# RWKV mixer's end on one core: batch-norm statistics, a two-part second output, a quarter of the output product in fp32, gate weights on strips

## The chip, the cores and the metric

The kernel runs on one core of a Trainium2 chip. The metric is the device time of one execution in microseconds (us); lower is better. The engines are named as in the profile: PE is TensorE (matrix products and transposes), DVE is VectorE, ACT is ScalarE, POOL is GpSimd, SP issues most DMAs. The program is fixed: every engine works through its own list of instructions in order and waits for semaphores of the others.

## The reference

Two layers over 256 positions of width 1024, all in float32: layer 0 mixes positions by sparse attention (NSA), layer 1 by RWKV-7, and each is followed by a squared-ReLU MLP of width 4096. The change lies at the end of the RWKV mixer and at its entrance. Cut to what matters there:

```python
def rwkv7_mixer(h, v_first, x_mix, w_rkv, ..., g1, g2, k_k, k_a, r_k, ln_w, ln_b, w_out, v_res):
    dx = jnp.pad(h, ((0, 0), (1, 0), (0, 0)))[:, :-1] - h
    xr, xw, xk, xv, xa, xg = (h + dx * x_mix[i] for i in range(6))
    ...
    g = jax.nn.sigmoid(xg @ g1) @ g2                      # 1024 -> 160 -> 1024
    def step(state, inp):                                 # one position after the other
        sa = jnp.einsum('bhij,bhj->bhi', state, -kk_t)
        state = state * w_t[...] + sa[..., None] * (kk_t * a_t)[...] + v_t[..., None] * k_t[...]
        return state, jnp.einsum('bhij,bhj->bhi', state, r_t)
    y = ...                                               # (1, 256, 16 heads, 64)
    mu = jnp.mean(y, axis=-1, keepdims=True)
    var = jnp.mean(jnp.square(y - mu), axis=-1, keepdims=True)
    yn = ((y - mu) * lax.rsqrt(var + GN_EPS)).reshape(B, S, D) * ln_w + ln_b
    y = yn + bonus.reshape(B, S, D)
    return (y * g) @ w_out, v_first
```

## The kernel before

The 256 positions lie as two token tiles, t = 0 and t = 1, of 128 rows each. Weights come from memory in 188 chunks of 512 KB (`wchunk`, L224): SP issues the load into a ring of four buffers `wst`, ACT copies it to `wh` in the shortened format fp32r (L231), and DVE subtracts to get the rest `wl` (L233). A product with weights is then three fp32r products (`mm3`, L265: high by high L267, high by low L268, low by high L269). Products that need no split are plain fp32 (`mm`).

A scheduler places the instructions of PE, ACT, DVE and POOL from the program as written, within their dependences; `tc.issue_after(x)` keeps what is built inside it behind x. SP's list stays as written. Large tiles live in numbered slots (`big`, `done`, L240) and PSUM accumulators in a pool of four (`pacc`).

**Entrance.** `mlp` (L376) ends with its second product for the last four of 32 f-steps (the tail), first for t = 0, then for t = 1 one column block `cb` after the other. After each block `x` is updated (L430) and `after(t, cb)` of `rwkv_input` (L816) runs: it normalises x, transposes it (tile `hnp`, L833), and DVE makes `hn` and the shifted difference `dx`. For t = 1 it also builds the small products of decay and a (`lora`, L804, tile `pl`) and of the gate (`lora_g`, L810, tile `pg`, 160 columns), the gate's for both token tiles as hn·g1 + dx·(mix·g1). Later the gate rows are transposed to `gT` (L907 to L916), 128 and 32 of the 160 in separate parts.

**Middle.** `rwkv` works in four chunks of 64 positions, C = 64. `products` (L1109) makes the masked products M of a chunk. `gate_gemm` (L1137) makes g by one 128-row and one 32-row fp32 product of 512 columns for each of four blocks. Then the recurrence, for each chunk c: right sides Z (`right_sides`, tile pZ, copied to `Zt` by ACT), solution Q (`solve`, tile pQ, to `VS` by ACT), next state S (`next_state`, tile pS; DVE adds `w` and scales to `W`), and after two chunks the output Y of a token tile (`output`, tile pY, to `y` by ACT). A string lists the order in which they are built (L1330).

**End.** `group_norm(t)` (L1283) works in two halves of 512 columns: DVE sums, scales and subtracts the mean; ACT squares; DVE sums again; POOL takes the power -1/2; DVE multiplies by it, by `lnw`, adds `vt` and multiplies by `g`. PE transposes the half (`yTp`, L1305); ACT makes `yTh` (L1307), DVE `yTl` (L1308). `out_proj` (L329, called at L1341) multiplies by w_out in eight chunks (kh, cb), quarter kh and column block cb, six products each for a token tile, into `roa`. The last three chunks go to slots as `rowh`, `rowl`. Then x is updated (L367) and the next MLP's input is transposed (`m1p`) and split (`m1h`, `m1l`); its first product is `mu`.

Of the kernel before, what the change touches and what calls it, by code (L numbers as in the profile page):

```python
# [9 lines left out]
F32 = mybir.dt.float32  # L10
# [11 lines left out]
H = 16  # L22
# [153 lines left out]
def trunk(ctx: ExitStack, tc: tile.TileContext, wb, x_in, wg, cw1k, cw1v, cw2, vecs_in, l1, w2, a2, g2, rows,  # L176
# [45 lines left out]
    wnext = [0]  # L222

    def wchunk(pattern=None, alloc=None, **dims):  # L224
# [8 lines left out]
        V.tensor_tensor(wl, st, wh.bitcast(F32), op=ALU.subtract)  # L233
# [95 lines left out]
    def out_proj(hT, lT, name, after, tail=TAIL, hold=(), own=2):  # L329
# [9 lines left out]
        def part(kh, cb, t):  # L339
            if (kh, cb) not in wch:  # L340
# [6 lines left out]
            wh, wl = wch[kh, cb]  # L347
            for k in range(2):
                kk = kh * 2 + k
                sl = slice(t * 128, (t + 1) * 128)  # L350
                mm3(acc[t, cb], hT(kk, sl), lT(kk, sl), wh[:, k], wl[:, k], kk == 0, kk == KT - 1)
# [8 lines left out]
        for t in range(NT):  # L360

            rest = sorted(od[-tail:], key=lambda o: (o[0] > 1 and o[1] + 1, o)) if t else od[-tail:]
            for i, (kh, cb) in enumerate(rest):
                part(kh, cb, t)
# [11 lines left out]
    def mlp(hl, name, after, early=lambda: None):  # L376
        h, l = hl
        with tc.tile_pool(name=f"mlp{name}", bufs=1) as mp:
# [44 lines left out]
            for t in range(NT):  # L423
                for cbs in ((0,), (1,)) if t else ((0, 1),):
                    with tc.issue_after(m_.ins) if t else ExitStack():
                        for f in range(NF - TAIL, NF):
                            m_ = second(f, t, cbs)
                    for cb in cbs:
                        xs = x[:, t, cb * 512:(cb + 1) * 512]
                        V.scalar_tensor_tensor(xs, acc[t][cb], r2[:, t:t + 1], xs, op0=ALU.mult, op1=ALU.add)  # L430
                        after(t, cb)
# [356 lines left out]
    def rwkv_input(wts):  # L788
# [27 lines left out]
        def after(t, cb_):  # L816
# [13 lines left out]
            for i in range(2):  # L830
                p = pmm([128, 4, 128], "hnp")
                for j in range(4):
                    nc.tensor.transpose(p[:, j], xs[t][:, (4 * i + j) * 128:(4 * i + j + 1) * 128], ident)  # L833
# [5 lines left out]
            if t == 1:  # L839
                lora_g(0)  # L840
                lora(1)
                lora_g(1)
                done(l1a, m1a, g1, m1g)
# [15 lines left out]
    def rwkv(inp):  # L859
        hn, dx, xrh, xrl, w2t, a2t, lo = inp  # L860
        with ExitStack() as es:
# [45 lines left out]
            gT = pool.tile([128, 2, S], F32, name="gT")  # L907
            gs = sm.tile([128, NT, 160], F32, tag="gs", bufs=1, name="gs")
            act(gs, lo["pg"], AF.Tanh, scale=0.5)
            V.tensor_scalar(gs, gs, 0.5, 0.5, op0=ALU.mult, op1=ALU.add)  # L910
            p = pacc("pgT", [128, 2, NT, 128])
            for t in range(NT):
                nc.tensor.transpose(p[:, 0, t], gs[:, t, :128], ident)
                nc.tensor.transpose(p[:32, 1, t], gs[:, t, 128:], ident)
            act(gT[:, 0].rearrange("p (t q) -> p t q", t=NT), p[:, 0], AF.Copy)
            act(gT[:32, 1].rearrange("p (t q) -> p t q", t=NT), p[:32, 1], AF.Copy)  # L916

            def feature_tile(hT, lT, dst):
# [5 lines left out]
                act(dst, p, AF.Copy)  # L924

# [9 lines left out]
            xvh, xvl = split(V_MV, "xv")  # L935
            done(hn, dx)
# [196 lines left out]
            nc.sync.dma_start(gw[1][:32], g2[128:])  # L1133
# [3 lines left out]
            def gate_gemm(t):  # L1137
                sl = slice(t * 128, (t + 1) * 128)
                for cb in range(2):
# [277 lines left out]
```

## Time and profile before

| what | value |
|---|---|
| three runs | 734.05, 734.08, 735.78 us; median 734.08 |
| profiled execution, its own time | 735.48 us |
| its span on the core | 733.70 us |
| mean granted clock of TensorE | 0.989 of full speed |
| PE busy | 711.5 us, 97% of the span |
| DVE, ACT, POOL busy | 468.8, 432.0, 18.2 us |
| chain that ended last | PE 91%, DVE 4%, ACT 2%, issue 1%, DMA 1% |

The span is the time from the core's first to its last instruction in the profiled execution; what lies around it makes up the rest of that execution's time. Times inside the trace count from the start of the span. A busy share is an average over stages with different limits, so what is idle in a stage is read from that stage. A row of a timeline gives the start, the length, engine, line, operation, tiles and shapes; in brackets stand the idle time of that engine just before and what ended it. Matrix products overlap, so the time that one costs is the step from its start to the next one's, which is shorter than its length.

### The profile page before, as it was taken

To read this page: it belongs to the slowest core of one execution; us is meant where nothing else is said; L and a number is where in the kernel's file an instruction comes from. 1 tells how busy PE (TensorE), PEld (TensorE's weight loads), DVE (VectorE), ACT (ScalarE), POOL (GpSimd) and SP (SyncE) were. 2 spreads that over 40 slices of the span, in tenths; PEclk is the share of its full clock that TensorE was granted. 3 is DMA by queue.
4 is the path that set the end of the run, shared out by engine and by line. 5 is a ranking of instruction groups with operands and counts; after the bars stand their busy time and mean duration, and the time that the engine had idled before them with its cause. 6 is when DMAs were issued, how large, how long until landed. Compare 5 with 4: busy or idle time off the path is not lost.

```text
span 733.7 us, 13437 instructions
## 1 busy us (share of the span) xinstructions
PE 711.5 (97%) x5308; PEld 609.1 (83%) x5308; DVE 468.8 (64%) x960; ACT 432.0 (59%) x863; POOL 18.2 (2%) x34
## 2 busy tenths in 40 slices
PE   9999999999999999999999999996899999999996
PEld 7877776779898999898999987685689998899894
DVE  5765899548545454566875889987657454545454
ACT  6735688328555555565366896765157556555652
POOL 1000000000000000000000010001200000000000
PEclk9999999999999999999999999999799999999999
DMA  7947120126755555575025423052318555555531
GB/s 288 336 153 272 37 79 2 59 87 232 235 176 195 179 193 177 192 240 200 1 87 173 145 65 87 3 191 84 132 58 255 192 185 184 191 185 187 185 103 58
DMA packets 32012, 111.52 MB, mean 152 GB/s; under 512 B 3629, under 2 KB 4141, under 8 KB 31950
## 3 DMA queue, kind: packets, MB, share of 16 engines
q1 hardware_dynamic: 30878, 108.95, 44.0%
q10 hardware_dynamic: 928, 1.19, 0.7%
q8 instruction: 42, 0.69, 0.4%
q0 software_dynamic: 144, 0.52, 0.2%
q14 instruction: 20, 0.16, 0.1%
HBM read 108.55 MB, written 1.05 MB: 149 GB/s over the span
## 4 chain that ended last, share of the span: by engine, by line
PE 91%; DVE 4%; ACT 2%; issue 1%; DMA 1%; POOL 0%; SPq 0%; POOLq 0%; DVEq 0%
PE mu L267 8%; PE mu L268 8%; PE mu L269 8%; PE mo L267 8%; PE mo L269 8%; PE mo L268 8%; PE acc L268 4%; PE acc L269 4%; PE acc L267 4%; PE pa L269 2%; PE pa L268 2%; PE pa L267 2%; PE S L639 2%; PE po L683 1%; PE pM L1116 1%
## 5 line engine op out<-in xcount | busy, mean ns | idle before, releaser
L233 DVE TENSOR_TENSOR wl<-wst,wh 128x1024 fp32r<-128x1024 f32 x175 | 213.6, 1224 | 181.3 <-ACT wh L231 181.0
L231 ACT ACTIVATE wh<-wst 128x1024 fp32r<-128x1024 f32 x175 | 184.6, 1060 | 161.2 <-PE mu L268 77.5
L267 PE MATMUL mo<-wh,mqh 128*128 128x512 f32 x224 | 88.5, 397 | 0.0
L268 PE MATMUL mo<-wl,mqh 128*128 128x512 f32 x224 | 88.4, 395 | 0.0
L269 PE MATMUL mo<-wh,mql 128*128 128x512 f32 x224 | 87.4, 396 | 0.0
L267 PE MATMUL mu<-m0h,wh 128*128 128x256 f32 x256 | 72.5, 285 | 0.4 <-DVE m0l L305 0.4
L269 PE MATMUL mu<-m0h,wl 128*128 128x256 f32 x256 | 72.3, 283 | 0.0
L268 PE MATMUL mu<-m1l,wh 128*128 128x256 f32 x256 | 72.0, 282 | 0.0
L268 PE MATMUL mu<-m0l,wh 128*128 128x256 f32 x256 | 71.8, 282 | 0.0
L269 PE MATMUL mu<-m1h,wl 128*128 128x256 f32 x256 | 71.7, 281 | 0.0
L267 PE MATMUL mu<-m1h,wh 128*128 128x256 f32 x256 | 71.3, 282 | 0.0
L269 PEld LDWEIGHTS mo<-wh,mql 128*128 128x128 f32 x224 | 42.1, 188 | 10.3
L267 PEld LDWEIGHTS mu<-m0h,wh 128*128 128x128 f32 x256 | 48.2, 189 | 1.8 <-DVE m0l L305 0.6
L268 PEld LDWEIGHTS mu<-m0l,wh 128*128 128x128 f32 x256 | 48.4, 189 | 1.3 <-DVE m0l L305 0.2
L268 PEld LDWEIGHTS mu<-m1l,wh 128*128 128x128 f32 x256 | 48.2, 188 | 1.2
L267 PEld LDWEIGHTS mu<-m1h,wh 128*128 128x128 f32 x256 | 47.8, 188 | 1.2
L268 PEld LDWEIGHTS mo<-wl,mqh 128*128 128x128 f32 x224 | 42.2, 188 | 8.0
L267 PEld LDWEIGHTS mo<-wh,mqh 128*128 128x128 f32 x224 | 42.1, 188 | 7.7
L269 PEld LDWEIGHTS mu<-m1h,wl 128*128 128x128 f32 x256 | 48.2, 188 | 0.0
L269 PEld LDWEIGHTS mu<-m0h,wl 128*128 128x128 f32 x256 | 48.1, 188 | 0.0
L267 PE MATMUL acc<-wh,n0h 128*128 128x512 f32 x80 | 31.9, 405 | 0.1
L268 PE MATMUL acc<-wl,n0h 128*128 128x512 f32 x80 | 31.3, 397 | 0.2 <-DVE wl L233 0.2
(369 smaller groups left out, 1444.9 us busy)
## 6 DMA issues: line engine op xcount, KB each, us to landing
wst<-in_wb_dram SPq DMA_DIRECT2D x188, 512.0 KB, 3.7
w1t<-in_cw1k_dram SPq DMA_DIRECT2D x4, 512.0 KB, 6.1
w1t<-in_cw1v_dram SPq DMA_DIRECT2D x4, 512.0 KB, 7.1
x<-in_x_dram SPq DMA_DIRECT2D x4, 256.0 KB, 4.9
VS<-vt ACTq DMA_DIRECT2D x8, 128.0 KB, 4.7
out_dram<-xg SPq DMA_DIRECT2D x4, 256.0 KB, 2.2
g<-in_l_dram SPq DMA_DIRECT2D x2, 320.0 KB, 5.9
l1a<-in_l_dram SPq DMA_DIRECT2D x1, 512.0 KB
```

The costliest lines, as they stand in the source:

```text
L231: act(wh, st, AF.Copy)
L233: V.tensor_tensor(wl, st, wh.bitcast(F32), op=ALU.subtract)
L267: mm(o, lh, rh, start=first, stop=False)
L268: mm(o, lh, rl, start=False, stop=False)
L269: return mm(o, ll, rh, start=False, stop=last)
L639: mm(S1, qT[gp][:, hg, 128:256], kT[gp][:, s], start=True, stop=True)
L683: mm(po[s * 64:(s + 1) * 64, :S], vv[:, 0, vs], pt0[s][:, b], start=False, stop=False)
L1116: mm(p[s][:, j], head(BK, k0 + j, s, c).rearrange("p a s -> p (a s)"), head(AR, k0 + j, s, c).rearrange("p a s -> p (a s)"), start=True, s ...
```

## The change

Seven parts. (1) In the MLP's tail the hnp transposes of t = 0 are placed ahead of the last two f-steps of (t = 1, cb = 1). (2) The gate's small product of t = 1 is made from `xg` = hn + mix·dx, eight DVE operations and eight products instead of sixteen; the gate rows are transposed later, the 32 narrow ones onto four strips of 32 rows. (3) `gate_gemm` lists the four full products and then the four 32-row ones, each in rows of its own. (4) The order string and the holds change, and Y of the second token tile is built in two parts with the first tile's group norm between. (5) Group norm takes its statistics by BN_STATS, eight of 64 columns for each half, and seven 128x8 operations; POOL makes the power and the bias; the normalisation is eight 64-column ACTIVATEs with scale and bias pointers, for t = 0's second half eight DVE TENSOR_SCALARs. (6) The last quarter of the output product (kh = 3) is plain fp32: its two chunks are not split, and `yTf` holds that quarter of y. (7) The holds on weight chunks move behind the statistics.

```diff
@@ out_proj
         def part(kh, cb, t):
+            if (kh, cb) not in wch and whole is not None and kh == 3:
+                wt = big([128, 2, 512], f"{name}w{cb}")
+                extra.append(wt)
+                nc.sync.dma_start(wt.rearrange("p k c -> p (k c)"), wb[wnext[0]])
...
+                if whole is not None and kh == 3:
+                    marks[kh, cb, t] = mm(acc[t, cb], whole[:, k, sl], wch[kh, cb][:, k], start=False, stop=kk == KT - 1)
+                    continue
@@ mlp
                         for f in range(NF - TAIL, NF):
-                            m_ = second(f, t, cbs)
+                            with tc.issue_after(amid.ins) if cbs == (1,) and amid and f >= NF - 2 else ExitStack():
+                                m_ = second(f, t, cbs)
@@ rwkv_input, after
                 lora(1)
-                lora_g(1)
@@ rwkv
+            def gate_rows():
...
+                p = pacc("pgT", [128, 3, 128])
+                for t in range(NT):
+                    nc.tensor.transpose(p[:, t], gs[:, t, :128], ident)
+                    for cb in range(2):
+                        q = 32 * (2 * t + cb)
+                        mm(p[q:q + 32, 2], gs[:, t, 128:], ident, start=True, stop=True)
+                act(gT, p, AF.Copy)
...
+            for k in range(KT):
+                V.scalar_tensor_tensor(xg[k // 4][:, k % 4], kt(dx, k)[:, 128:], vcol(V_MG, k), kt(hn, k)[:, 129:],
+                                       op0=ALU.mult, op1=ALU.add)
+            for k in range(KT):
+                mm(lo["pg"][:, 1], xg[k // 4][:, k % 4], kt(lo["g1"], k), start=k == 0, stop=k == KT - 1)
...
-                    mm(p, gT[:, 0, sl], gw[0][:, cs], start=True, stop=False)
-                    mm(p, gT[:32, 1, sl], gw[1][:32, cs], start=False, stop=True)
-                    act(g[t][:, cs], p, AF.Copy)
+                for q in range(4):
+                    mm(p[q], gT[:, q // 2], gw[0][:, 512 * (q % 2):512 * (q % 2) + 512], start=True, stop=False)
+                for q in range(4):
+                    mm(p[q], gT[32 * q:32 * q + 32, 2], gw[1][32 * q:32 * q + 32, :512], start=False, stop=True)
+                for q in range(4):
+                    act(g[q // 2][:, 512 * (q % 2):512 * (q % 2) + 512], p[q], AF.Copy)
@@ group_norm
-                    V.tensor_reduce(gst[:, t, hs], yh, axis=AX.X, op=ALU.add)
-                    V.tensor_scalar(gst[:, t, hs], gst[:, t, hs], 1.0 / DH, None, op0=ALU.mult)
-                    V.tensor_tensor(yh, yh, gst[:, t, hs][:, :, None].to_broadcast([128, 8, DH]), op=ALU.subtract)
-                    act(sq, yh, AF.Square, scale=DH ** -0.5)
-                    V.tensor_reduce(gst[:, t, hs], sq, axis=AX.X, op=ALU.add)
...
+                    with tc.issue_after(st_done[1].ins) if t == 0 else ExitStack():
+                        for h in range(8):
+                            V.bn_stats(bst[:, h], y_[:, (8 * i + h) * DH:(8 * i + h + 1) * DH])
...
+                        last["stat"] = V.tensor_scalar(rsd, rsd, 1.0 / DH, GN_EPS, op0=ALU.mult, op1=ALU.add)
+                    P.tensor_tensor(rsd, rsd, neg_half[:, 0:1].to_broadcast([128, 8]), op=ALU.pow)
+                    P.tensor_tensor(nb, bs_, rsd, op=ALU.mult)
+                    with tc.issue_after(st_done[2].ins) if t == 0 and i else ExitStack():
+                        for h in range(8):
+                            yh = y_[:, (8 * i + h) * DH:(8 * i + h + 1) * DH]
+                            if t == 0 and i:
+                                V.tensor_scalar(yh, yh, rsd[:, h:h + 1], nb[:, h:h + 1], op0=ALU.mult, op1=ALU.add)
+                            else:
+                                with tc.issue_after((last["tail"] if t else last["VS", 2]).ins):
+                                    act(yh, yh, AF.Identity, scale=rsd[:, h:h + 1], bias=nb[:, h:h + 1])
...
+                    n = 2 if i else 4
+                    last["yTh"] = act(oh[i][:, :n, sl], p[:, :n], AF.Copy)
+                    last["yTl"] = V.tensor_tensor(ol[i][:, :n, sl], p[:, :n], oh[i][:, :n, sl].bitcast(F32), op=ALU.subtract)
+                    if i:
+                        last["tail"] = act(of[:, :, sl], p[:, 2:], AF.Copy)
@@ order and holds
-            for o in "Z0 B1 Q0 M2 S0 m2 Z1 B2 M3 g0 g1 Q1 S1 Y0 N0 Z2 Q2 S2 Z3 Q3 Y1".split():
+            for o in "Z0 B1 Q0 M2 S0 m2 Z1 M3 Q1 B2 S1 g0 g1 Y0 N0 Z2 Q2 S2 Z3 Q3 Y1".split():
...
-                           hold=[early] * 3 + [(st_done[2].ins, last["VS", 3].ins)])
+                           hold=[(last["stat"].ins, last["VS", 1].ins)] * 2 + [(last["o"].ins, last["VS", 3].ins)]
+                           + [[i_.ins for i_ in last["head"]] + [last["yc"].ins]], whole=of, marks=last)
```

What the scheduler makes of it is read from the built order. First PE at the gate product (pg is the accumulator, gw the gate's second weights, gT the transposed gate rows); L1169 is the full product and L1171 the 32-row one in the changed kernel:

```order
L1144 MATMUL pM<-AR_4516,BK_4517 128x128
L1169 MATMUL pg_4853<-gw_4818,gT 128x512
L1171 MATMUL pg_4853<-gw_4819,gT 128x512
L1169 MATMUL pg_4854<-gw_4818,gT 128x512
L1171 MATMUL pg_4854<-gw_4819,gT 128x512
L1169 MATMUL pg_4855<-gw_4818,gT 128x512
L1171 MATMUL pg_4855<-gw_4819,gT 128x512
L1169 MATMUL pg_4856<-gw_4818,gT 128x512
L1171 MATMUL pg_4856<-gw_4819,gT 128x512
L1183 MATMUL pKB<-cst,BK_4212 128x128
```

The two kinds alternate, as L1142 and L1143 do before; only the accumulator's number and the rows of gT and gw differ.

Second, DVE around the state of the third chunk (w and W of `next_state`; y the first token tile's output), of the kernel before:

```order
L1291 TENSOR_REDUCE gst<-y_5425 128x8
L1261 TENSOR_TENSOR W_5190<-w,F 128x256
L1291 TENSOR_REDUCE gst<-y_5425 128x8
L1292 TENSOR_SCALAR gst<-gst 128x8 x2
L1293 TENSOR_TENSOR y_5425<-y_5425,gst 128x512 x2
L1295 TENSOR_REDUCE gst<-ysq_5486 128x8 x2
L1296 TENSOR_SCALAR gst<-gst 128x8 x2
L1260 TENSOR_TENSOR w<-pS,W_5190 128x256
L1298 TENSOR_TENSOR y_5425<-y_5425,gst 128x512
L1261 TENSOR_TENSOR W_5190<-w,F 128x256
L1299 TENSOR_TENSOR y_5425<-y_5425,lnw 128x512
L1260 TENSOR_TENSOR w<-pS,W_5190 128x256
```

and of the changed kernel (bst, bs, nb, rsd are the statistics, their sum, bias and scale; 16 BN_STATS and nine small operations stand ahead of the first row shown, and ahead of those w, W, w, W of the second chunk):

```order
L1325 TENSOR_TENSOR bs_5749<-bst_5748 128x8
L1324 TENSOR_TENSOR nb_5751<-nb_5751 128x8
L1327 TENSOR_SCALAR bs_5749<-bs_5749 128x8
L1326 SCALAR_TENSOR_TENSOR rsd_5750<-nb_5751,rsd_5750 128x8
L1328 TENSOR_SCALAR rsd_5750<-rsd_5750 128x8
L233 TENSOR_TENSOR wl_5798<-wst_5794,wh_5796 128x1024
L233 TENSOR_TENSOR wl_5810<-wst_5806,wh_5808 128x1024
L1287 TENSOR_TENSOR w<-pS,W_5196 128x256
L1288 TENSOR_TENSOR W_5196<-w,F 128x256
L1287 TENSOR_TENSOR w<-pS,W_5196 128x256
L1288 TENSOR_TENSOR W_5196<-w,F 128x256
L1340 TENSOR_TENSOR y_5430<-y_5430,lnw 128x512
```

The four operations of w and W have moved together, and the work on y that stood between them stands behind; two splits of weights have moved ahead of them.

Third, PE where the first token tile's output product ends in the changed kernel (roa the accumulators of the two column blocks, row the unsplit chunk):

```order
L269 MATMUL roa_5793<-rowh,yTl_5490 128x512
L357 MATMUL roa_5792<-row_5866,yTf 128x512 x2
L1346 MATMUL yTp<-cst,y_5636 128x128 x4
L357 MATMUL roa_5793<-row_5923,yTf 128x512 x2
L301 MATMUL m1p<-cst,x 128x128 x4
L1346 MATMUL yTp<-cst,y_5636 128x128 x4
L267 MATMUL roa_5981<-wh_5796,yTh_5487 128x512
```

Before, the eight transposes yTp and the eight m1p stand in two blocks behind the last roa product of the tile; now they stand in halves around the fp32 products L357.

## Rows read from the trace of the kernel before

**Rows 1.** The page: busy time by engine, and its costliest DVE group.

```profile
PE 711.5 (97%) x5308; PEld 609.1 (83%) x5308; DVE 468.8 (64%) x960; ACT 432.0 (59%) x863; POOL 18.2 (2%) x34
...
L233 DVE TENSOR_TENSOR wl<-wst,wh 128x1024 fp32r<-128x1024 f32 x175 | 213.6, 1224 | 181.3 <-ACT wh L231 181.0
```

**Rows 2.** TensorE's waits, 486 to 546 us: total us, times, longest.

```profile
PE roa L267 <- ACT yTh L1307: 4.0, 1, 4.0
PE pZ L1234 <- DVE W L1261: 2.4, 3, 1.6
...
PE roa L269 <- DVE yTl L1308: 0.6, 1, 0.6
```

**Rows 3.** Stretches: busy us of PE, PEld, DVE, ACT, POOL; granted clock; DMA.

```profile
494.00:504.00 10.00, 6.32 (x168) 5.26 (x166) 8.57 (x20) 3.29 (x8) 3.26 (x2) 1.00 0.32 104
...
512.00:516.00 4.00, 0.22 (x1) 0.22 (x2) 3.93 (x6) 2.88 (x6) 0.00 (x0) 0.67 0.90 293
516.00:524.00 8.00, 7.40 (x18) 5.33 (x19) 7.73 (x16) 0.84 (x2) 4.41 (x3) 0.52 0.56 200
```

**Rows 4.** PE timeline, output product: start, length, line, tiles, shapes, idle before.

```profile
515.78 0.79 PE L267 MATMUL roa<-wh,yTh 128*128 128x512 f32 x1 [3.98 <-ACT yTh L1307]
...
516.80 0.63 PE L267 MATMUL roa<-wh,yTh 128*128 128x512 f32 x1
517.23 0.63 PE L268 MATMUL roa<-wl,yTh 128*128 128x512 f32 x1
...
524.16 0.40 PE L267 MATMUL roa<-wh,yTh 128*128 128x512 f32 x1
524.39 0.40 PE L268 MATMUL roa<-wl,yTh 128*128 128x512 f32 x1
```

**Rows 5.** PE timeline at the mixer's entrance.

```profile
348.23 0.49 PE L807 MATMUL pl<-hn,l1a 128*128 128x128 f32 x2 [0.57 <-DVE hn L834]
...
349.42 0.49 PE L808 MATMUL pl<-dx,m1a 128*128 128x128 f32 x2 [0.43 <-DVE dx L836]
...
354.83 0.44 PE L814 MATMUL pg<-m1g,dx 128*128 128x160 f32 x2
355.11 0.43 PE L813 MATMUL pg<-g,hn 128*128 128x160 f32 x2
```

**Rows 6.** PE timeline at the gate product.

```profile
457.34 1.12 PE L1142 MATMUL pg<-gw,gT 128*128 128x512 f32 x2
458.40 1.12 PE L1143 MATMUL pg<-gw,gT 32*128 32x512 f32 x2
```

**Rows 7.** DVE timeline in the recurrence.

```profile
490.58 0.42 DVE L1260 TENSOR_TENSOR w<-pS,W 128x256 f32<-128x256 f32 x1
...
499.43 0.42 DVE L1260 TENSOR_TENSOR w<-pS,W 128x256 f32<-128x256 f32 x1 [0.91 <-PE pS L1256]
...
502.09 0.68 DVE L1298 TENSOR_TENSOR y<-y,gst 128x512 f32<-128x512 f32 x1
502.69 0.68 DVE L1300 TENSOR_TENSOR y<-y,vt 128x512 f32<-128x512 f32 x1
```

**Rows 8.** DVE groups by shape, 335 to 546 us: busy us, mean ns.

```profile
L1292 DVE TENSOR_SCALAR gst<-gst 128x8 f32<-128x8 f32 x4 | 0.6, 169 | 0.0
...
L1176 DVE TENSOR_TENSOR Tb<-Tb,pd 128x65 f32<-128x65 f32 x1 | 0.2, 224 | 0.0
```

**Rows 9.** ACT timeline: bonus scaling, then VS and Zt of the recurrence.

```profile
458.28 3.92 ACT L1100 ACTIVATE vt<-vt,bon 128x64 f32<-128x64 f32 x16
...
497.49 1.57 ACT L1247 ACTIVATE VS<-pQ 64x256 f32<-64x256 f32 x4
504.54 0.66 ACT L1236 ACTIVATE Zt<-pZ 128x256 f32<-128x256 f32 x2 [5.47 <-PE pZ L1234]
```

**Rows 10.** ACT groups by shape, 335 to 546 us: busy us, mean ns.

```profile
L1002 ACT ACTIVATE th<-th,hk 128x256 f32<-128x256 f32 x8 | 4.4, 618 | 0.0
```

**Rows 11.** POOL timeline, group norm's powers.

```profile
498.53 3.26 POOL L1297 TENSOR_TENSOR gst<-gst,neg_half 128x8 f32<-128x8 f32 x2 [65.57 <-DVE gst L1296]
```

More of the change, by code (lines that the diff above doesn't have):

```diff
@@ L1311, in more @@
+                    if i:
+                        last["tail"] = act(of[:, :, sl], p[:, 2:], AF.Copy)
+                    else:
+                        last["head"] = last["yTh"], last["yTl"]
+                    yield
+                done(y_, g[t], vt[t])
             def more(c):
@@ L1325, in out_of @@
                 y.append(big([128, D], f"y{t}"))
-                output((2 * t, 2 * t + 1), y[t])
-            ysqs = []
-            for o in "Z0 B1 Q0 M2 S0 m2 Z1 B2 M3 g0 g1 Q1 S1 Y0 N0 Z2 Q2 S2 Z3 Q3 Y1".split():
+                part = output((2 * t, 2 * t + 1), y[t])
+                next(part)
+                if t:
+                    norm = group_norm(0, y[0])
+                    next(norm)
+                    with tc.issue_after(last["tr"].ins):
+                        next(part)
+                    next(norm)
@@ L1331, in rwkv @@
+                for _ in part:
+                    pass
+                if t:
+                    next(norm, None)
+            for o in "Z0 B1 Q0 M2 S0 m2 Z1 M3 Q1 B2 S1 g0 g1 Y0 N0 Z2 Q2 S2 Z3 Q3 Y1".split():
                 if o[0] == "N":
                     oh, ol = halves("yTh", F32R, hi=True), halves("yTl", F32R, hi=True)
-                    ysqs.append(big([128, H, DH], "ysq0"))
+                    of = sm.tile([128, 2, S], F32, name="yTf")
                     continue
                 c = int(o[1])
-                with tc.issue_after(st_done[0].ins if o[0] in "mg" else first.ins):
+                with tc.issue_after(st_done[0].ins if o[0] in "mg" else last["S"].ins if o == "Y0" else first.ins):
@@ L1343, in rwkv @@
+                           + [[i_.ins for i_ in last["head"]] + [last["yc"].ins]], whole=of, marks=last)
             next(out)
[L1344 removed]
             done(AR, Wt)
             next(out)
[L1347 to L1350 removed]
+            norm = group_norm(1, y[1])
+            next(norm)
+            with tc.issue_after(last["tr"].ins):
+                next(out)
+            for _ in norm:
+                pass
@@ L1351, in rwkv @@
+            for _ in out:
+                pass
             done(oh, ol)
```

96 lines of the change are left out of this document (46 added, 50 removed).

## The prediction

> **What bounds the kernel now.** I read the page of the profile first. TensorE is busy for 711.5 of 733.7 us [rows 1], so a change of two or three places can win only what TensorE waits there, what it runs at half clock, and work taken off it. The list of TensorE's waits for the stretch of the change (486 to 546 us) names three of weight: 4.0 us for the scalar engine's yTh before the output product, 2.4 us in three waits for VectorE's W inside the recurrence, and 0.6 us for yTl [rows 2]. The table by stretches then shows what the long wait costs afterwards: from 512 to 516 TensorE does 0.22 us of work while the granted clock falls to a mean of 0.67, and from 516 to 524 it works at 0.52, which is the lower of its two levels (1.2 against 2.4 GHz) [rows 3]. The timeline prices it: 512-column products follow each other every 0.43 us there and every 0.23 us at 524 [rows 4]. Last I read the input stage, where TensorE waits 0.57 and 0.43 us behind the hnp transposes [rows 5].
>
> All sums are made against the profiled execution, 735.48 us (span 733.70 and 1.78 around it). That is 1.40 us above the median of the three runs, 734.08; I carry the difference, not the profiled time, over to the median.
>
> **Input stage.** The hnp transposes of the first token tile now stand two f-steps before the end of the MLP's last output block, so products cover the wait for hn and dx: -1.00 us (0.57 + 0.43). lora_g(1), 16 products of 160 columns, becomes 8; the step between two of them is 0.27 us (354.83, 355.11) [rows 5]: -2.2. The eight multiply-adds xg that replace the other half go to VectorE, some 0.3 us each (128 columns, between 0.22 for 65 and 0.42 for 256 [rows 7, 8]), beside the first r and k products that TensorE has queued; without that cover they would cost 2.4. Two more gate transposes (six for four) cost 0.2. But the second hnp group now stands behind all of lora_g(0), so the same two waits return there, and with less work between them: from 1.0 (as before) to 2.0 us; I take 1.5. Sum -1.5, bounds -2.0 and -0.9.
>
> **Gate product.** A full-height product takes 1.06 us (457.34 to 458.40), and the 32-row product behind it is as long, 1.12 against 1.12 [rows 6]. The source lists four full products and then four strips in different row groups, but the built order still alternates full, strip, full, strip. The scheduler undid the grouping, so no two strips are neighbours: 0 us. The Trainium skill, "TensorE: Matmul & The Clock Gate", Part 3 (Packing small matmuls), states that 32-row products in distinct row groups run concurrently, four of them 3.07 times as fast as in turn. Its page "TensorEngine Tiling (Array Packing)", Key Properties, adds that a change of the tiling mode drains the engine. By that figure four neighbouring strips would take 4.2 / 3.07 = 1.4 us instead of 4.2, an estimate, and the sum below would be -9.7. By the order, which makes no strip a neighbour of another, it stays -6.9.
>
> **Recurrence.** Before, DVE's queue has three wl and reductions among the first W pieces, and y's normalisation between the second ones: the half that ends at 503.7 stood behind two such operations (502.09, 502.69) and cost 1.65 us [rows 7]. Now w, W, w, W stand together, twice, with all statistics of the first tile and two wl between the pairs. Do these fit? Without the wl between, the first four end near 490.8 in this trace's time (w ran at 490.58 behind a wl of 1.22, four take 0.34 each), and the next pS releases w at 499.43 [rows 7]. Into 8.6 us go 14 small 128x8 operations (0.17 us long [rows 8], some 0.14 apart: 2.0), two wl (1.22 long [rows 1], 1.14 apart: 2.3) and 16 BN_STATS. BN_STATS is in no row. Below it cannot be less than a 128x8 operation's step, 0.12; above I take the length of a 128x256 operation, 0.42 [rows 7]. A 128x65 tensor_tensor takes 0.22 long [rows 8], a step of some 0.15 when the next is independent, and BN_STATS reads as many columns: 0.15. The 16 cost 2.4, the block ends at 497.5, and W waits for pS alone. A second W one step after the first still makes TensorE wait about 0.5. So waits of 2.4 become some 0.7: -1.7, bounds -2.2 and +0.7 (at 0.42 the block ends at 501.8, 2.4 late).
>
> The normalisation of the first half goes to ACT, eight 64-column ACTIVATEs with two pointers ahead of Zt. With one pointer 16 of them took 3.92 us, 0.245 each [rows 9]; with two pointers only 128x256 is shown, 0.618 [rows 10]. I take 0.35, that is 2.8 us behind the VS that ends at 499.1 (497.49 and 1.57), so 501.9. Zt began at 504.54 [rows 9]; less the W waits that go, 2.1, it is wanted at 502.4: free. At 0.6 each Zt would be 1.5 late. POOL gives nb in time: two powers of 1.63 (3.26 for two) [rows 11] and one small product from 493.0 on, about 497.
>
> **The gap before the output product.** The 3.98 us for yTh came from ACT's queue: conversions and the square of y stood before it; then 0.60 for yTl [rows 2]. Now there is no square, yTh of half 0 stands right behind the first two copies of the second Y part, and the last two chunks need no conversion. What is late next is yTl: VectorE ends the second W pair at 500.8 (499.43 and four times 0.34), the first tile's y at 505.6 (six operations of 0.60, as 502.09 to 502.69 [rows 7], and eight of 0.15), a wl at 507.3 (its wh comes only behind the third VS), eight BN_STATS at 508.5, five small ones at 509.2 and yTl at 509.9. TensorE, ready at 511.8 before (515.78 less 3.98 [rows 4]), is ready 1.7 earlier and 0.4 more, since it no longer waits for the copy of y: 509.7 less what the parts overlap, about 509.2. So 4.6 becomes 1.0, with the time that a signal takes: -3.6, bounds -4.3 and -1.9.
>
> **The fp32 quarter.** Eight fp32 products of 512 columns at 1.06 [rows 6] replace 24 at 0.233 [rows 4]: 8.4 - 5.6 = +2.8, on TensorE with nothing to hide it. The conversions it saves (two ACT, two DVE) are only cover.
>
> **Second tile.** yTf waits on ACT for VectorE's yTl of half 1, which stands behind three splits of weights, and the 16 scalings of the second tile queue behind yTf. By this count y of half 0 is ready at the time that the first fp32 pair ends: +0.3, bounds 0 and 2.5.
>
> **The clock.** Between 515.8 and 523.3 sixteen products ran at 0.43 instead of 0.23 [rows 4]. With waits of about 1 us instead of 4 I expect the full clock: -3.2, or 0 if it falls all the same.
>
> Sum: -1.5 - 1.7 - 3.6 + 2.8 + 0.3 - 3.2 = -6.9. That is 728.6 profiled, and 727.2 for the median.
>
> **Rivals.** *The clock falls again.* The waits in a row around 494 to 510 (W, Zt, VS, then yTl) leave TensorE less busy than anywhere; speaking for it is the 0.67 after such a stretch, against it that 494 to 504 had only 6.32 us busy of 10 and kept 1.00 [rows 3]. Without the term: 730.4.
> *The strips do overlap*, across the full products between them. Then three of four 1.05 us strips vanish: -3.2, 724.0. Against it: the order, and full products that occupy all rows. The rule of the Trainium skill quoted above speaks of strips beside strips alone.
> *Many small operations cost more than the few wide ones: slower.* Place: DVE ahead of the second W pair, and ACT ahead of the third Zt. Price: BN_STATS at 0.42 adds 2.4 at W, 2.2 ahead of yTl (eight of 0.27) and as much in the second tile; ACT scalings at 0.6 make Zt 1.5 late; and with such waits the clock term of 3.2 is lost. Together +11.5: 738.7. It decides from a BN_STATS step above 0.27, where 16 of them no longer fit before pS; up to 0.27 it costs under 2 us. For it: every operation of this kind has a fixed part, the 128x8 one still takes 0.17 [rows 8]. Against it: the nearest row by columns is 0.22 long [rows 8].
>
> **How the numbers follow.** Forecast 0.62, with its own range 724.5 to 730; clock alone 0.18; strips 0.06; small operations 0.14, half of it slower, half near no change, since its price comes in parts. A measurement of this kernel tells 0.3%, 2.2 us, from no change: faster is below 731.9, slower above 736.3. Faster: 0.62, strips 0.06 and most of the clock case, 0.15, together 0.83; same: 0.03 and 0.07, 0.10; slower: 0.07. The range, 722.0 to 733.0, reaches past the strips below and past the clock case above, and leaves out most of the last rival.
>
> **What would show it.** Right: TensorE's waits list without yTh, with a yTl wait of about 1 us; W waits under 1 us together; granted clock 1.00 from 505 to 520; eight roa products at about 1.06; the gate's eight products still 8.4 us; hnp before the last mo, and one new wait for hn and dx behind the second hnp. Wrong: BN_STATS spaced over 0.27, W waits over 2 us, Zt waiting behind scalings on ACT, y of the second tile late by more than 2 us, or a clock near 0.5 under the first roa products.

## The result and the profile after

The changed kernel takes 725.67 us (median of four runs, 725.18 to 726.17); the kernel before took 734.93 beside it (734.05 to 735.93, four runs). The ratio is 0.9879, with an interval from 0.9863 to 0.9894: faster by 1.2%, and 1.5 us below the forecast of 727.2, inside its range. The profiled execution is 725.32 us, its span 723.4, where before had 735.48 and 733.70.

The page's line on TensorE, to be set beside [rows 1], says that its busy time fell by 6.8 us, so most of the gain is work or clock and not waiting.

```profile
PE 704.7 (97%) x5290; PEld 600.4 (83%) x5290; DVE 466.1 (64%) x1010; ACT 437.0 (60%) x882; POOL 20.9 (3%) x38
```

TensorE's waits after (340 to 546 us: total us, times, longest) answer to [rows 2, 5]: yTh and W are gone, yTl is left, and Zt, the second tile's y and the second hnp group are new or longer.

```profile
PE pQ L1271 <- ACT Zt L1263: 1.7, 2, 1.2
PE roa L267 <- DVE yTl L1350: 1.7, 1, 1.7
PE yTp L1346 <- DVE y L1342: 1.7, 3, 0.8
PE pZ L1257 <- DVE TT L1232: 0.8, 1, 0.8
PE pl L823 <- DVE dx L851: 0.7, 1, 0.7
...
PE pl L822 <- DVE hn L849: 0.3, 1, 0.3
```

The table by stretches after (columns as in [rows 3]) shows the full granted clock in every stretch. Where the kernel before did 0.22 us of TensorE work in four, while yTh was late, there are now 2.29 in four, and no stretch at 0.52 follows.

```profile
428.00:432.00 4.00, 4.00 (x62) 3.11 (x61) 3.34 (x7) 3.87 (x14) 1.90 (x2) 1.00 0.22 85
494.00:504.00 10.00, 8.52 (x237) 7.35 (x234) 8.32 (x20) 7.27 (x18) 0.89 (x3) 1.00 0.33 109
504.00:508.00 4.00, 2.29 (x11) 1.76 (x12) 3.90 (x27) 3.77 (x6) 1.32 (x1) 1.00 0.92 321
508.00:512.00 4.00, 4.00 (x19) 3.20 (x18) 3.95 (x10) 0.09 (x1) 2.28 (x3) 1.00 0.50 198
```

One row of before was not among those read for the prediction. It belongs beside the first of these: before ran four microseconds of the products of v, the last of the three products r, k and v, at a mean of 0.57.

```profile
428.00:432.00 4.00, 4.00 (x12) 3.05 (x11) 3.57 (x11) 3.22 (x12) 0.95 (x1) 0.57 0.55 190
```

TensorE's timeline at the output product after, to be set beside [rows 4]: products 0.23 apart from the start, pairs of fp32 products in 1.72 (517.73 to 519.45), and two waits for y of the second tile.

```profile
506.28 0.50 PE L267 MATMUL roa<-wh,yTh 128*128 128x512 f32 x1 [1.71 <-DVE yTl L1350]
506.62 0.39 PE L268 MATMUL roa<-wl,yTh 128*128 128x512 f32 x1
506.85 0.40 PE L269 MATMUL roa<-wh,yTl 128*128 128x512 f32 x1
...
517.26 0.63 PE L1346 MATMUL yTp<-cst,y 128*128 128x128 f32 x4 [0.60 <-DVE y L1342]
517.73 1.88 PE L357 MATMUL roa<-row,yTf 128*128 128x512 f32 x4
519.45 0.60 PE L301 MATMUL m1p<-cst,x 128*128 128x128 f32 x4
520.87 0.63 PE L1346 MATMUL yTp<-cst,y 128*128 128x128 f32 x4 [0.82 <-DVE y L1342]
```

Rows at the entrance and the gate after, to be set beside [rows 5, 6]: the waits for hn and dx stand behind the second hnp now; the gate still alternates full and strip, 1.06 from one to the next.

```profile
356.69 0.49 PE L822 MATMUL pl<-hn,l1a 128*128 128x128 f32 x2 [0.35 <-DVE hn L849]
357.88 0.49 PE L823 MATMUL pl<-dx,m1a 128*128 128x128 f32 x2 [0.71 <-DVE dx L851]
...
453.96 1.12 PE L1169 MATMUL pg<-gw,gT 128*128 128x512 f32 x2
455.02 1.12 PE L1171 MATMUL pg<-gw,gT 32*128 32x512 f32 x2
```

Timelines of DVE, ACT and POOL after, in order of time, to be set beside [rows 8, 9, 11]: eight BN_STATS in 1.11 us, ACT's scalings 0.345 apart once POOL has made `nb`, and in the second tile sixteen scalings behind `yTf`, which itself waits 4.12 us for `yTl`.

```profile
487.92 1.11 DVE L1320 BATCH_NORM_STATS2 bst<-y 128x6 f32<-128x64 f32 x8 [0.84 <-ACT y L1306]
...
490.31 3.97 POOL L1329 TENSOR_TENSOR rsd<-rsd,neg_half 128x8 f32<-128x8 f32 x2 [59.12 <-DVE rsd L1328]
...
494.49 2.76 ACT L1338 ACTIVATE y<-y,nb,rsd 128x64 f32<-128x64 f32 x8 [0.91 <-POOL nb L1330]
...
497.29 0.69 DVE L1340 TENSOR_TENSOR y<-y,lnw 128x512 f32<-128x512 f32 x1 [1.52 <-ACT y L1338]
...
511.91 0.39 ACT L1352 ACTIVATE yTf<-yTp 128x256 f32<-128x256 f32 x1 [4.12 <-DVE yTl L1350]
512.19 5.41 ACT L1338 ACTIVATE y<-y,nb,rsd 128x64 f32<-128x64 f32 x16
```

Where the time of the two profiled executions went, by the starts of TensorE's instructions:

| stretch | how it is read (before, after) | difference | forecast |
|---|---|---|---|
| entrance, with the products of r and k | first product of v 427.73, 425.93 | -1.80 | -1.5 |
| products of v, up to the gate | 427.73 to 457.34, 425.93 to 453.96; the 0.57 stretch is absent after | -1.58 | none |
| gate | 457.34 to 465.77, 453.96 to 462.39 | 0 | 0 |
| recurrence | gate's end to "ready for roa": 465.77 to 511.80, 462.39 to 504.57 | -3.85 | -1.7 |
| gap before roa | 3.98 + 0.60, 1.71 | -2.87 | -3.6 |
| clock | 16 products 0.43 apart, now 0.23 | -3.2 | -3.2 |
| fp32 quarter | 8 products of 0.86 in place of 24 of 0.233 | +1.3 | +2.8 |
| second tile | new waits of 0.60 and 0.82 | +1.4 | +0.3 |

These come to -10.6. The start of `mu`, the next MLP's first product, moved from 545.36 to 534.95, by -10.4, and the profiled times differ by 10.16. The 0.2 between the sum and `mu` was not followed.

### The profile page after: what moved, and what is told of

Same layout as the page of the kernel before. It is cut to its first block, busy times and chain, and to the rows that moved or that the text cites. A ratio compares the mean times of both kernels' runs of the same rounds, so it can differ in the third digit from the quotient of the medians.

```text
span 723.4 us, 13471 instructions
## 1 busy us (share of the span) xinstructions
PE 704.7 (97%) x5290; PEld 600.4 (83%) x5290; DVE 466.1 (64%) x1010; ACT 437.0 (60%) x882; POOL 20.9 (3%) x38
## 3 DMA queue, kind: packets, MB, share of 16 engines
HBM read 108.69 MB, written 1.05 MB: 152 GB/s over the span
## 4 chain that ended last, share of the span: by engine, by line
PE 83%; DVE 9%; ACT 4%; issue 2%; DMA 1%; SPq 0%; POOLq 0%; POOL 0%; DVEq 0%; ACTq 0%
PE mu L267 9%; PE mu L268 8%; PE mu L269 8%; PE mo L267 8%; PE mo L269 8%; PE mo L268 8%; PE acc L268 2%; PE acc L269 2%; PE acc L267 2%; PE S L654 2%; PE pa L268 2%; PE pa L267 2%; PE pa L269 2%; DVE pd L1201 2%; DVE Tb L1204 1%
```

## The experiments

Each kernel is the changed one with the edit shown. Times are medians with their lowest and highest run, and a time given as one execution is a single run; ratios are against the kernel before, run beside it. One value in particular is used below: the distance from the start of the first tile's second group of transposes (yTp) to the start of `mu`, which is 31.03 us in the changed kernel (503.92 to 534.95).

### Are strips that stand together concurrent, and is that worth anything? (e1)

```
-  for q in range(4): mm(p[q], ... 32-row strip ...)
+  with tc.issue_after(full.ins):
+      for q in range(4): mm(p[q], ... 32-row strip ...)
```

> The changed kernel with its four 32-row gate products held behind the four full ones, so that they are neighbours in distinct rows. In the changed kernel the eight alternate and take 8.43 us (453.96 to 462.39), 1.05 each, while the fp32 products of the output product, all of full height, take 0.86 each (1.72 for two). Theory A (the strips overlap when they are neighbours): the eight take under 5.5 us. Theory B (a change of tile height costs 0.2 each time, strips do not overlap): about 7.0 us. Theory C (fp32 products of this form simply take 1.05): 8.4 us. For the time: TensorE already waits 0.81 us for VectorE's TT before the first Z, so whatever the gate product gains should come back as a longer wait there: span within 0.6 us of the changed kernel's 723.4; the rival is that the gain (1.4 to 3.5 us) shows in full.

Measured: 726.78 us (725.36 to 727.50), ratio 0.9893 (0.9876 to 0.9910). TensorE's timeline, and its table by stretches:

```profile
455.47 3.70 PE L1169 MATMUL pg<-gw,gT 128*128 128x512 f32 x8
459.10 1.14 PE L1172 MATMUL pg<-gw,gT 32*128 32x512 f32 x8
460.91 1.15 PE L1184 MATMUL pKB<-cst,BK 128*128 128x128 f32 x8 [0.67 <-ACT g L1174]
...
464.39 3.63 PE L1222 MATMUL pU<-T,LO 32*32 32x32 f32 x128 [2.33 <-DVE T L1207]
```

```profile
460.00:464.00 4.00, 1.39 (x12) 0.84 (x8) 3.83 (x19) 3.30 (x8) 0.00 (x0) 0.97 0.00 0
464.00:470.00 6.00, 5.61 (x146) 5.55 (x148) 5.90 (x6) 2.36 (x4) 0.00 (x0) 0.50 0.01 3
```

The four strips take 1.14 us together, and a full product 0.91 (3.63 for four) instead of 1.06. The gate takes 4.8 us instead of 8.4. The rule quoted in the prediction from the Trainium skill ("TensorE: Matmul & The Clock Gate", Part 3, Packing small matmuls) would have given about 1.4 us for the strips, an estimate; this trace agrees that they overlap, and is somewhat faster. The Trainium skill, "TensorEngine Tiling (Array Packing)", Key Properties, states that a change of the tiling mode drains the engine; the 0.15 that a full product loses beside a strip is in line with that, but no run isolates it. And the time does not fall. TensorE then waits 2.33 us for VectorE's T and 0.67 for ACT's g, and the following stretch runs at 0.50, the lower of its levels. From the end of the products of v (452.94) to the first pZ (473.32) it takes 20.38 us, in the changed kernel 19.14 (451.43 to 470.57): the 3.7 us that the gate gave are used up by these waits and by the slower products. So the gate product was cover for VectorE's work, and the forecast's 0 was right for a second reason that it did not have. How much would be left at the full clock no run shows.

### The entrance alone (e3), and the order string (e7)

```
-  with tc.issue_after(amid.ins) if cbs == (1,) and amid and f >= NF - 2 else ExitStack():
+  with ExitStack():
```

> The changed kernel with the hnp transposes of the first token tile behind the whole MLP tail again (only part 1 undone). Theory A (the waits for hn and dx come back where they were and those behind the second hnp stay): TensorE waits 0.5 and 0.4 us after the first hnp and 0.35 and 0.71 after the second, and the first r product begins 1.0 us later. Theory B (the scheduler puts other products there): the sum of the four waits stays near 1.1 and the time does not change.

One execution, 725.27 us. The waits stand behind the first hnp only, 0.6 for hn and 0.4 for dx, instead of 0.35 and 0.71 behind the second:

```profile
PE pl L822 <- DVE hn L849: 0.6, 1, 0.6
PE pl L823 <- DVE dx L851: 0.4, 1, 0.4
```

The products of v begin at 425.89 against 425.93. The placement of hnp moves 1.0 us of waiting from one place to the other, and part 1 of the change shows no gain. That leaves the halved gate product for the -1.80 of this stretch, where the forecast's own sum has -2.2 for it and +0.2 for the transposes; no run takes it back alone.

```
-  for o in "Z0 B1 Q0 M2 S0 m2 Z1 M3 Q1 B2 S1 g0 g1 Y0 ...
+  for o in "Z0 B1 Q0 M2 S0 m2 Z1 B2 M3 g0 g1 Q1 S1 Y0 ...
```

> The changed kernel with the order string of before (key rows of chunk 2, masked products of chunk 3 and the gates ahead of Q1 and S1). From the gate product's end to the second yTp the changed kernel takes 42.0 us where the kernel before takes 45.8 to the end of its yTp. Theory A (the order of building makes part of that gain): 43 us or more, with S1 later and TensorE waiting for W. Theory B (the gain comes from the work removed between w and W and from the holds on the weight chunks, and the scheduler finds the same order): within 0.4 us of 42.0.

One execution, 727.49 us, with 1.6 us of it in a half-clock stretch at 428 that the string cannot touch. From the gate's end to the second yTp it takes 41.9 us against 41.5, and the W waits stay away. So it is not the string that made them go. Left are the holds on the splits and the work taken out between w and W; no run separates these two.

### Is the quarter in fp32 worth its price? (e2)

All four quarters split in three products as before; the second tile's last part keeps its place.

```
-  if whole is not None and t == 0 and i == len(rest) - 1:
+  if tail == 8 and t == 0 and i == len(rest) - 1:
-  n = 2 if i else 4
+  n = 4
-  last["tail"] = act(of[:, :, sl], p[:, 2:], AF.Copy)
+  last["tail"] = last["yTh"]
-  ... whole=of, marks=last)
+  ... marks=last)
```

> The changed kernel with the last quarter of the output product in three fp32r products again, its two chunks split, and yTh and yTl of full width; everything else as changed. Theory A (the prediction's price: fp32 at 1.05): TensorE has 2.8 us less to do there, and the whole gets faster by up to that. Theory B (the changed trace's price, 0.86): 1.3 us less. Theory C: the quarter was worth more than its price, because two conversions on ACT (1.06 each) and two on DVE (1.22 each) come back and yTl of the second half grows from 0.42 to 0.68, so the second token tile's y is later: then the waits before yTp, 1.4 us now, grow past 2.5 and the time is the same or longer.

Measured: 727.43 us (725.77 to 727.99), ratio 0.9903 (0.9885 to 0.9920). From the first roa product to `mu` it takes 28.85 us, with the quarter 28.67: TensorE is spared 1.3 us of products. Of this 0.8 returns as waits (2.2 us of them between the first product and the second tile's last yTp, where the changed kernel has 1.4). The second half of the second tile's y is ready 18.08 us after the start of the first tile's second yTp, in the changed kernel 16.80: 1.28 later, as much as TensorE was spared. The waits, 500 to 546 us, behind the first one:

```profile
PE m1p L301 <- DVE x L378: 1.5, 2, 1.1
PE yTp L1346 <- ACT y L1338: 0.7, 1, 0.7
PE roa L269 <- DVE yTl L1350: 0.3, 1, 0.3
```

What the quarter saves is conversions and splits on ACT and VectorE, and TensorE waits for what stands behind them. On TensorE alone it looks like a loss of 1.3; on the stretch it costs nothing (28.67 against 28.85), and the times of the two kernels overlap.

### What does the wait for yTl cost, and does the clock matter there? (e4, e6)

e4 adds five reductions of yTp, which nothing uses, ahead of the first yTl. e6 puts the second tile's BN_STATS behind it.

```
+  if t == 0 and i == 0:                      # e4
+      for _ in range(5): d_ = V.tensor_reduce(dm, p, axis=AX.X, op=ALU.add)

-  with tc.issue_after(st_done[1].ins) if t == 0 else ExitStack():      # e6
+  with tc.issue_after(st_done[1].ins if t == 0 else last["head0"].ins):
```

> The changed kernel with five reductions of 0.60 us, whose result nobody uses, put in VectorE's list right before yTl of the first tile's first half, so that TensorE's wait before the first roa product grows from 1.71 to about 4.7 us. In the changed kernel the products behind that wait run at the full clock (0.23 us apart); in the run with yTf on VectorE they ran at half clock for 3.3 us behind the same wait of 1.71. Theory A (the wait is what lowers the clock, and the longer it is the surer): the first roa products are 0.43 apart for 3 us or more, and mu begins about 3.0 + 1.5 to 3.2 us later, less what the second tile's waits (1.4) give back. Theory B (the clock there has nothing to do with the wait): products 0.23 apart, mu about 1.6 to 3.0 later.

> The changed kernel with the second token tile's BN_STATS held behind yTl of the first tile's first half. In the changed kernel TensorE waits 1.71 us for that yTl at the first roa product, and VectorE runs eight BN_STATS (1.11) and five small operations (0.5) right before it. Theory A (VectorE's order sets the gap): the wait falls to about 0.1 us. As the statistics then end 0.7 us later and TensorE arrives 1.6 us earlier, the waits before yTp of the second tile grow by about 2, and the time changes by less than 0.6 us. Theory B (these waits have slack): 1.6 us faster.

e4, one execution: 729.70 us. The wait is 5.30 us, and products follow 0.43 apart behind it, as before:

```profile
510.98 0.76 PE L267 MATMUL roa<-wh,yTh 128*128 128x512 f32 x1 [5.30 <-DVE yTl L1357]
511.54 0.63 PE L268 MATMUL roa<-wl,yTh 128*128 128x512 f32 x1
511.97 0.63 PE L269 MATMUL roa<-wh,yTl 128*128 128x512 f32 x1
```

But the distance from yTp to `mu` grows by 3.50 (34.53), nearly the 3.59 that the wait grew by. The lower clock adds nothing to it: the waits for the second tile's y, 1.42, are gone in its place.

e6: 725.55 us (724.89 to 725.93), ratio 0.9878 (0.9863 to 0.9893). The list of waits has none for yTl. The distance is 31.02, the same to 0.01. Of the 1.6 us by which TensorE begins the output product earlier, 0.71 is lost around a new wait of 0.35 for rowl, and 0.87 to longer waits for the second tile's y (with the 0.26 ahead of the first tile's, 2.6 in all):

```profile
PE yTp L1346 <- DVE y L1342: 2.6, 3, 1.5
```

So a wait removed at roa gains nothing, and VectorE's work added there is paid for in full.

### What sets the second tile? (e5, e8, e10, e11)

In e5 VectorE copies yTf, so ACT's scalings no longer queue behind it. e8 is e5 and e6 together, with POOL's transfer of gf behind its biases. e10 is e8 with all statistics of the second tile built ahead of the last three splits. e11 is the changed kernel again, beside e10.

```
-  last["tail"] = act(of[:, :, sl], p[:, 2:], AF.Copy)             # e5
+  V.tensor_copy(of[:, :, sl], p[:, 2:])
+  last["tail"] = last["yTh"]

+  with tc.issue_after(nb_done[-1].ins):                           # e8, besides
       P.dma_start(gf, ...)

+  ready = [stats(0), stats(1)]                                    # e10, besides
+  late.append(last["stat"].ins)          # holds the splits of chunks 3 to 5
```

> The changed kernel with the copy yTf made by VectorE behind yTl instead of by ACT. In the changed kernel ACT stands idle 4.12 us in front of yTf, with the 16 scalings of the second token tile queued behind it, and TensorE then waits 0.60 and 0.82 us before the two yTp groups of that tile. Theory A (the queue behind yTf sets these waits): the scalings start at about 510.3, when POOL has nb, and both waits go: 1.4 us faster. Theory B (POOL's power and bias, with the issue of gf's DMA between them, set them): at most the second wait shrinks, under 0.6 us faster.

e5: 726.63 us (725.10 to 727.15), ratio 0.9890 (0.9873 to 0.9907). Both waits for the second tile's y are gone, but not by the copy alone. In this execution the clock fell behind the same 1.71 us wait:

```profile
508.00:512.00 4.00, 4.00 (x11) 3.14 (x12) 3.97 (x18) 1.45 (x4) 3.61 (x3) 0.57 0.63 249
```

That made TensorE 1.53 us late. The first half of y is ready 9.74 us behind the start of the first yTl, against 11.57, so that wait would have gone in any case. The second half comes 0.66 earlier, and by these times most of its wait of 0.82 would have stood without the slower products. The distance is 30.76.

> The changed kernel with three moves together: the second tile's BN_STATS behind the first yTl (this took the 1.71 us wait away, and the waits before yTp of the second tile grew from 1.4 to 2.3), yTf copied by VectorE instead of ACT (this took the waits before yTp of the second tile away), and the issue of gf's DMA on POOL behind the last bias of group norm. Theory A (the two gains add once both are made): no wait before roa and at most 0.6 us before the second tile's yTp, from first roa to mu at most 28.2 us (28.67 in the changed kernel), and from the end of the v product to mu 81.7 us (83.84 there): about 2.1 us faster than the changed kernel, 723.5. As the wait of 1.71 is gone, no product of roa runs at half clock. Theory B (POOL's two powers and biases set the second tile whatever the queue on ACT): waits of 2 us or more stay and the gain is under 0.6 us.

e8: 725.93 us (723.88 to 726.45), ratio 0.9860 (0.9837 to 0.9882), distance 30.40. A new wait of 1.62 us for x has come. The timelines of POOL, ACT and DVE show the chain ahead of it: the power of the second half starts only at 514.37, since its input stands behind three splits on DVE; ACT scales from 516.69, DVE goes on at 519.48, and x stands behind that. Neither expectation was met in full: the new wait is under 2 us, and the distance is only 0.6 shorter.

```profile
514.37 2.00 POOL L1329 TENSOR_TENSOR rsd<-rsd,neg_half 128x8 f32<-128x8 f32 x1 [3.44 <-DVE rsd L1328]
...
516.69 2.76 ACT L1338 ACTIVATE y<-y,nb,rsd 128x64 f32<-128x64 f32 x8 [2.95 <-POOL nb L1330]
...
519.48 0.69 DVE L1340 TENSOR_TENSOR y<-y,lnw 128x512 f32<-128x512 f32 x1 [3.15 <-ACT y L1338]
```

> All statistics of the second token tile are built ahead of the three splits that e8 left between them and the second yTl of the first tile (yTf on VectorE, gf's transfer behind the biases, as in e8). Theory A: what sets the end is VectorE's list from the first tile's second yTp to the second tile's y: in after, e3, e5, e6 and e7 the distance from that yTp to the first mu is 30.8 to 31.0 us whatever TensorE waits on the way, and 34.5 in e4 with 3.6 us more on VectorE. In e8 the power of the second half stands behind the splits (514.37), so ACT scales it from 516.69 and VectorE waits 3.15. Without that the power is ready some 3.5 us earlier, the second half follows the first on ACT, m1p's wait of 1.6 goes, a wait of up to 0.7 for rowl comes: distance 29.3 to 29.9, time 724.0 to 725.2. Theory B: POOL and ACT are no part of it, or the later splits cost TensorE as much: distance 30.4 or more, time 725.5 to 726.5, the same as the changed kernel.

> The changed kernel once more, beside e10 on the same chip in the same rounds, so that the two can be told apart: 725.7 by its four runs (725.18 to 726.17). Theory A of e10 puts it 0.5 to 1.7 us above e10, theory B level with it. Its profile also shows once more whether the clock falls behind the 1.71 us wait for yTl: it did in e3, e5 and e7, not in after and e2. By theory A (VectorE's list sets the end) the distance from the first tile's second yTp to mu is 30.8 to 31.1 in either case; if the clock decides, it is 32.3 or more where the clock falls.

e10: 724.44 us (723.24 to 724.76), ratio 0.9863 (0.9837 to 0.9888). e11, in the same rounds: 726.00 us (724.53 to 727.90), ratio 0.9893 (0.9871 to 0.9914). The two intervals overlap; of the runs, two of e10's four lie above the lowest of e11's six, and none above the second lowest (725.24). The profile is clearer than the times: distance 28.60 against 31.02 in e11, shorter than the 29.3 to 29.9 that was expected. The chain of e8 has dissolved (power 2.8 us earlier, both halves scaled in one go), and 0.8 us of waits are left between 500 and 546:

```profile
510.29 2.37 DVE L233 TENSOR_TENSOR wl<-wst,wh 128x1024 fp32r<-128x1024 f32 x2
...
511.54 2.61 POOL L1336 TENSOR_TENSOR rsd<-rsd,neg_half 128x8 f32<-128x8 f32 x1
511.61 5.62 ACT L1345 ACTIVATE y<-y,nb,rsd 128x64 f32<-128x64 f32 x16 [1.82 <-POOL nb L1337]
...
517.26 0.69 DVE L1347 TENSOR_TENSOR y<-y,lnw 128x512 f32<-128x512 f32 x1 [0.70 <-ACT y L1345]
...
518.72 0.69 DVE L1349 TENSOR_TENSOR y<-y,g 128x512 f32<-128x512 f32 x1
```

```profile
PE m1p L301 <- DVE x L378: 0.3, 1, 0.3
PE yTp L1353 <- DVE y L1349: 0.3, 1, 0.3
PE roa L268 <- DVE wl L233: 0.2, 1, 0.2
```

Its profiled execution lost 1.8 us earlier, between the end of the r, k and v products and the second yTp (1.5 us of waiting for TT where the changed kernel has 0.8, and a mean clock of 0.72 from 470 to 474). There the lists of TensorE, VectorE and ACT stand exactly as in the changed kernel; why e8 and e10 both lost it was not settled. By its median e10 is the fastest version of this study, but the times alone do not show it faster than the changed kernel.

The distances side by side (us; the waits for the second tile are those of yTp, in e8 that of m1p, in e2 of both; in e4 most of 508 to 512 is the wait itself):

| kernel | wait for yTl | granted clock 508 to 512 | waits in the second tile | distance to mu |
|---|---|---|---|---|
| changed | 1.71 | 1.00 | 1.42 | 31.03 |
| e11, the same | 1.70 | 1.00 | 1.42 | 31.02 |
| e1 | 1.70 | 1.00 | 1.42 | 31.02 |
| e2 | 1.70 | 1.00 | 1.86 | 31.21 |
| e3 | 1.71 | 0.65 | 0 | 30.76 |
| e5 | 1.71 | 0.57 | 0 | 30.76 |
| e7 | 1.70 | 0.57 | 0 | 31.04 |
| e6 | 0 | 1.00 | 2.29 | 31.02 |
| e4 | 5.30 | 0.85 | 0 | 34.53 |
| e8 | 0 | 1.00 | 1.62 | 30.40 |
| e10 | 0 | 1.00 | 0 | 28.60 |

Wait and clock trade places and the distance hardly moves. What sets it in most of them is the way over VectorE's splits and statistics, POOL's powers and ACT's scalings to the second tile's y. That can be read from the end of the last operation on its second half, in the changed kernel

```profile
520.04 0.68 DVE L1342 TENSOR_TENSOR y<-y,g 128x512 f32<-128x512 f32 x1
```

that is 16.80 us behind the start of the distance. It is 16.78 to 16.80 in e1, e6, e7 and e11 as well, and the last yTp follows within 0.15. In e3 and e5 y is ready at 16.33 and 16.15, and there the slower products are what brings TensorE only at 16.71. In e8, at the full clock, y is ready at 16.16; in e10 at 13.49, and TensorE comes at 14.10 without a wait. In e4, with 3.6 us more on VectorE, it is 20.29.

## Why the prediction was right, step by step

The forecast was -6.9 on the profiled time, and the profiles differ by -10.16; between the medians beside each other it was -9.3. The direction and the places were right, and several sizes were not: against the forecast the gap before the output product (+0.7) and the second tile (+1.1) came out worse, the entrance (-0.3), the recurrence (-2.15) and the fp32 quarter (-1.5) better, and -1.58 came that had no term. That the median lies only 1.5 us below the forecast is in part luck: the profiles miss it by 3.3.

**Entrance, gate.** As forecast: -1.80 for -1.5, and 0 for 0. The waits returned behind the second hnp group at 1.06 us, not the 1.5 that was taken. The rival of overlapping strips fell as the prediction said: no strip is a neighbour of another, and each keeps its step of 1.05. e1 shows that they do overlap when they are neighbours, and that it brings nothing here.

**Recurrence: mis-sized, -3.85 for -1.7.** The prediction's own times have TensorE ready 2.6 earlier (511.8 to 509.2); its sum carries only the 1.7 of the W waits. The mechanism at w and W was right. BN_STATS costs 0.14 (eight in 1.11, 1.15 to the next operation), where 0.15 was taken, and a small operation mostly 0.09 where 0.14 was taken. The block before the second W pair ended at 493.92, just when pS released w, and the W waits went to nothing rather than to 0.7. Three more lines of before, of its waits from 340 to 546 us, belong beside this:

```profile
PE pQ L1244 <- ACT Zt L1236: 1.1, 2, 0.5
PE pT L1202 <- issue: 0.9, 1, 0.9
PE pS L1256 <- ACT VS L1247: 0.6, 1, 0.6
```

The VS wait and the issue gap of 0.9 are gone as well. The scalings on ACT cost 0.345 each, where 0.35 was taken. What was called free was not: POOL's two powers took 3.97 us instead of 3.26 [rows 11], the scalings began 0.91 late, and TensorE wanted Zt earlier because W no longer held it. It waits 1.22 for the last Zt, where before had 0.53. With that and 0.81 for TT, new in this profile and between 0.7 and 1.9 in the later ones that keep the alternating gate product, all waits of TensorE from the gate's end to "ready for roa" fell from 5.42 to 3.56 us, by 1.87. The other 2.0 are not waiting: the same products follow each other more closely, those of Y alone by 1.6. The prediction has no term for this, and what spaced them before was not followed.

**Gap before the output product: -2.87 for -3.6.** The mechanism was right: yTh off ACT's queue, then yTl late. The wait is 1.71, not 1.0; VectorE itself waits 1.52 us for the scalings of the first half, and its own eight scalings of the second half take 0.22 each (497.89 to 499.68), where 0.15 was taken.

**Clock: -3.2, as forecast in this profile, but by luck, and the term does not add up with the next.** Behind the same wait of 1.7 us the clock held in the changed kernel's two profiles, in e1 and in e2, and fell in e3, e5 and e7. In e5 the lists of TensorE, VectorE and ACT up to that wait are those of the changed kernel, so the list of instructions does not decide it. Where it fell, the second tile's waits were gone and the distance was 30.76 to 31.04. The rival "the clock falls again" priced that at 3.2 us; by e7 it costs nothing, since the second tile's y is late in either case. Only where y comes earlier does some of it show: e5 takes 0.36 more than e8, which has the same y at the full clock and 30.40.

**fp32 quarter: mis-sized, +1.3 for +2.8.** The price of 1.06 was read from the gate [rows 6], where every product changes between 128 and 32 rows. Products of one height take 0.86 here, and 0.91 in e1. e2 shows the term to be about 0 for the stretch.

**Second tile: mis-sized, +1.4 for +0.3.** The queue named in the prediction (yTf behind yTl of half 1, scalings behind yTf) is what happened; the count of its length was too short. The sum of both waits lies within the bounds that were given (0 to 2.5).

**Not in the forecast: -1.58.** Before ran part of the products of v at a mean of 0.57 of the clock, the changed kernel at 1.00. The profiles of e1, e5 and e7, which are alike there, have the low stretch again (a mean of 0.80, 0.76 and 0.76 in that window) and e2, e3, e4, e6 have not. So with the changed list it comes and goes between executions, and nothing shows that the change took it away; whether it also comes and goes in the kernel before, its one profile does not show. The medians contain it in unknown shares.

**The slower rival** needed a BN_STATS step above 0.27; it is half of that.

## What to carry to other kernels

Terms that are read at one engine (its wait, its clock, its products) add up only until another engine's list decides; then a wait that is removed or a clock that is kept comes back as the next wait, and one distance between two fixed points shows it at once. Price a product from a row with the same neighbours, not only the same shape. Where many engines hand over small pieces, put the inputs of the slowest one (here POOL's power) ahead of long work that can wait.

## What the runs showed of the hardware that was not expected

- Four fp32 products of 32 rows and 512 columns in different rows took 1.14 us together; in alternation with full products each took a step of 1.05. A full product took 0.91 beside full ones and 1.06 beside strips.
- Sixteen BN_STATS of 64 columns and fourteen 128x8 operations took 3.6 us on VectorE (487.92 to 491.56), where 4.4 had been reckoned.
- Two powers of 128x8 on POOL took 3.97 us here, 3.26 before; the second tile's took 1.63 to 2.61 each, depending on the kernel. What makes the difference was not tried.
- After the same wait of 1.7 us the granted clock stayed at 1.00 in some executions and fell to 0.50, the lower level, for some 3 us in others (a mean of 0.57 to 0.65 from 508 to 512). What decides it stays open.
